# Moving 32 columns between the last two pieces of the last row of a ReLU row-sum

## The chip, the cores and the metric

The kernel runs on one core of one Trainium2 chip. The metric is the device time of one execution in microseconds; most numbers are medians over several executions. The profiler's own span, from the first to the last instruction, is about 1.4 us shorter than that time.

## The reference, cut to what matters

```python
x = np.random.randn(32, 512, 1024).astype(np.float32)     # 67.11 MB
out = np.sum(np.maximum(x, 0), axis=-1)                   # 32 x 512
```

There are 16384 rows of 1024 numbers. Each of the 128 partitions takes 128 rows.

## The kernel before: the parts that matter here

SP (SyncE) issues all loads: seven large chunks of 16 rows a partition, then the tail of 8, 4, 2 and 1 rows, and at last the last row in three pieces.

```python
TAIL = [8, 4, 2, 1]
LAST = [512, 256, 256]
...
n0, n1 = LAST[0], LAST[0] + LAST[1]
parts = [buf[:, tb, r, 0:n0], buf[:, tb, r, n0:n1], last[:, 0 : LAST[2]]]
for k, (lo, hi) in enumerate([(0, n0), (n0, n1), (n1, D)]):
    sp.dma_start(out=parts[k], in_=xv[-1][:, BIG - 1, lo:hi]).then_inc(...)
sp.wait_ge(s_fact, 1)                                      # the early store
sp.wait_ge(s_fdve, 1)
sp.dma_start(out=ov[1][:, :], in_=res[:, start[1] : start[2]]).then_inc(s_store, 16)
sp.wait_ge(s_turn, 1)
sp.dma_start(out=of[0:P]..., in_=turned[0:P:32, 0:32]).then_inc(s_store, 16)
```

ScalarE (ACT) sums the first piece and VectorE (DVE) the second. Each puts its partial sum into one of two extra columns behind the third piece, so that DVE's last sum adds the third piece and both partial sums in one instruction:

```python
n = LAST[2]
act.wait_ge(s_in[-3], 16)
on_act(parts[0], last[:, n : n + 1]).then_inc(s_part, 1)
dve.wait_ge(s_in[-2], 16)
on_dve(parts[1], last[:, n + 1 : n + 2]).then_inc(s_part, 1)
dve.wait_ge(s_part, 2)
dve.wait_ge(s_in[-1], 16)
on_dve(last[:, :], res[:, J - 1 : J]).then_inc(s_tdve, 1)
sp.wait_ge(s_tdve, 1)                                      # the final store
sp.dma_start(out=ov[-1][:, :], in_=res[:, start[-1] : J]).then_inc(s_out, 16)
```

## Time and profile before

| | before |
|---|---|
| time, median of 3 (range) | 160.97 us (160.97 to 161.2) |
| span in the profile | 159.9 us |
| read rate over the span | 420 GB/s |
| busy share of DVE and of ACT | 76% and 63% |
| end of the last sum to end of span | about 1.5 us |

The way to read it is from the end: the chain of work that ended last says which wait released the last sum, and the timeline of the last 3 us says how near the other waits were. The prediction below shows both, with its lines.

### The profile page before, as it was taken

The numbers are of one execution on the slowest core, as the hardware profiler recorded it, in microseconds if no ns is written. First come the engines' busy times: TensorE is split into PE (matmuls) and PEld (weight loads), VectorE is DVE, ScalarE is ACT, GpSimd is POOL, SyncE is SP. The second block draws the span as 40 slices with busy tenths as digits, with TensorE's granted clock in tenths as the row PEclk, the third lists the DMA queues.
The fourth block names the chain that finished last, engine by engine and source line by source line (L and its number), as shares of the span: only waits on it lengthen the run. The fifth ranks groups of instructions, "written<-read, shape, count | busy, mean of one in ns | idle before, by whom it ended". The sixth has DMA issues, their size and how long they took to land.

```text
span 159.9 us, 150 instructions
## 1 busy us (share of the span) xinstructions
DVE 121.5 (76%) x58; ACT 101.4 (63%) x55; POOL 0.2 (0%) x4
## 2 busy tenths in 40 slices
DVE  0000000999959999999969989699899999598995
ACT  3000059990799709996099942999339980496974
POOL 0000000000000000000000000000000000000000
DMA  9979996996996996997989969969969969899994
GB/s 377 492 338 400 492 525 262 525 525 262 525 525 262 525 525 262 525 459 328 525 361 426 525 262 525 525 262 525 525 262 525 525 262 525 369 418 393 408 381 148
DMA packets 2457, 67.18 MB, mean 420 GB/s; under 512 B 536, under 2 KB 792, under 8 KB 1176
## 3 DMA queue, kind: packets, MB, share of 16 engines
q1 hardware_dynamic: 2456, 67.18, 98.0%
q14 instruction: 1, 0.01, 0.0%
HBM read 67.11 MB, written 0.07 MB: 420 GB/s over the span
## 4 chain that ended last, share of the span: by engine, by line
DMA 68%; ACT 18%; DVE 11%; SPq 1%; issue 0%
DMA buf<-in_x_dram 68%; ACT buf L137 18%; DVE res L152 11%; SPq L98 1%; SPq L106 0%; DVE buf L122 0%; DVE last L122 0%
## 5 line engine op out<-in xcount | busy, mean ns | idle before, releaser
L152 DVE TENSOR_REDUCE res<-buf 128x7 f32<-128x7168 f32 (+4 forms) x16 | 100.0, 6281 | 33.7 <-ACT buf L137 33.7
L137 ACT ACTIVATE buf<-buf 128x7168 f32<-128x7168 f32 (+4 forms) x16 | 80.7, 5099 | 45.9 <-DMA buf<-in_x_dram 45.9
L119 ACT ACTIVATE buf<-buf 128x1024 f32<-128x1024 f32 (+1 forms) x19 | 19.0, 1000 | 9.3 <-DMA buf<-in_x_dram 9.3
L122 DVE TENSOR_SCALAR_CACHE_REDUCE buf<-buf 128x1024 f32<-128x1024 f32 (+2 forms) x19 | 20.9, 1147 | 3.1 <-DMA buf<-in_x_dram 2.9
L119 ACT ACTIVATION_READ_ACCUMULATOR buf<-buf 128x1 f32 x19 | 3.5, 186 | 0.0
L137 ACT ACT_TABLE_LOAD x1 | 1.3, 1283 | 1.3 <-PEq L216 1.3
L122 DVE DVE_READ_ACCUMULATOR buf<-buf 128x1 f32 x19 | 1.6, 84 | 0.0
L122 DVE TENSOR_SCALAR_CACHE_REDUCE last<-last 128x258 f32<-128x258 f32 x1 | 0.4, 422 | 0.0
L161 DVE STREAM_TRANSPOSE turned<-res 128x32 f32<-128x32 f32 x1 | 0.2, 211 | 0.0
L185 DVE TENSOR_TENSOR res<-half 128x1 f32<-128x1 f32 x1 | 0.2, 160 | 0.1
L216 POOL MEMSET const-bfloat16-1.0<- 128x1 bf16 x1 | 0.1, 102 | 0.0
L216 POOL MEMSET const-uint8-127<- 128x1 uint8 x1 | 0.1, 101 | 0.0
L216 POOL MEMSET const-float32-0.0<- 128x1 f32 x1 | 0.1, 99 | 0.2 <-issue 0.2
L216 POOL MEMSET const-float32-1.0<- 128x1 f32 x1 | 0.1, 98 | 0.0
L122 DVE DVE_READ_ACCUMULATOR last<-last 128x1 f32 x1 | 0.1, 83 | 0.0
## 6 DMA issues: line engine op xcount, KB each, us to landing
buf<-in_x_dram SPq DMA_DIRECT2D x1, 7680.0 KB, 21.2
buf<-in_x_dram SPq DMA_DIRECT2D x1, 4096.0 KB, 26.8
buf<-in_x_dram SPq DMA_DIRECT2D x1, 2048.0 KB, 31.3
buf<-in_x_dram SPq DMA_DIRECT2D x2, 512.0 KB, 18.9
buf<-in_x_dram SPq DMA_DIRECT2D x1, 1024.0 KB, 33.3
buf<-in_x_dram SPq DMA_DIRECT2D x1, 256.0 KB, 34.5
buf<-in_x_dram SPq DMA_DIRECT2D x1, 128.0 KB, 34.4
last<-in_x_dram SPq DMA_DIRECT2D x1, 128.0 KB, 34.2
```

What stands on the lines that cost most here:

```text
L98: sp.dma_start(out=buf[:, tb, r : r + n, :], in_=xv[-1][:, r : r + n, :]).then_inc(s_in[NBIG + i], 16)
L119: return act.activation(t, t, AF.Relu, accum_out=acc)
L122: return dve.tensor_scalar(out=t, in0=t, scalar1=0.0, scalar2=None, op0=ALU.max, op1=ALU.add, accum_out=acc)
L137: act.activation(t, t, AF.Relu).then_inc(s_act, 1)
L152: dve.tensor_reduce(out=res[:, c * BIG + r : c * BIG + r + n], in_=buf[:, c % NB, r : r + n, :], axis=X, op=ALU.add,).then_inc(s_dve, 1)
L161: dve.transpose(out=turned[:, :], in_=res[:, 0:32]).then_inc(s_turn, 1)
L185: dve.tensor_tensor(out=res[:, j0 + r : j0 + r + 1], in0=half[:, 0:1], in1=half[:, 1:2], op=ALU.add)
L216: nc = _bacc.Bacc("TRN2", target_bir_lowering=False, num_devices=1)
```

## The change

The intent is to let DVE begin and end its own part of the last row a little earlier, at the price of a longer last sum. That would pay if DVE's own part is what the last sum waits for.

```diff
-LAST = [512, 256, 256]
+LAST = [512, 224, 288]
```

## The prediction

> **What bounds the kernel now.** I read the page first, for its chain of work that ended last (part 4), then that chain in order of time, then the timeline of the last three microseconds, and last the groups of instructions with different shapes kept apart. The page gives the share of the whole span:
>
> ```profile
> ## 4 chain that ended last, share of the span: by engine, by line
> DMA 68%; ACT 18%; DVE 11%; SPq 1%; issue 0%
> ...
> HBM read 67.11 MB, written 0.07 MB: 420 GB/s over the span
> ```
>
> The reader is to see that the kernel is one stream of 67.11 MB. Its rate over the span of 159.9 us, 420 GB/s, is nearly the same in every stretch that I cut out of it (419 in the first 20 us, 446 from 40 to 80, 419 from 80 to 120), and the busy share of the 16 DMA engines is 97% to 103% in all of them up to 145 us. ACT (ScalarE) and DVE (VectorE) have idle time, 63% and 76% busy. So nothing that the change does can matter except in two places: the bytes (they stay the same) and the tail, after the stream has run dry. The end of the chain in order of time:
>
> ```profile
> 123.13 34.38 DMA buf<-in_x_dram
> 157.51 0.02 issue
> 157.53 0.44 DVE buf L122 x2
> 157.97 0.02 issue
> 158.00 0.43 DVE last L122 x2
> ```
>
> The columns are start, length and what, in us. The transfer that was issued at 123.13 is the second piece of the last row (256 columns). It lands at 157.51, DVE sums it in 0.44 us (the sum and the read of its accumulator), then sums the third piece in 0.43 us. After that only the store is left: issue at 158.45, landing 1.4 us later. The timeline of the same stretch shows who else could have held up that last sum:
>
> ```profile
> 157.17 0.63 ACT L119 ACTIVATE buf<-buf 128x512 f32<-128x512 f32 x1
> 157.27 0.16 DVE L185 TENSOR_TENSOR res<-half 128x1 f32<-128x1 f32 x1
> 157.53 0.42 DVE L122 TENSOR_SCALAR_CACHE_REDUCE buf<-buf 128x256 f32<-128x256 f32 x1
> 157.70 0.19 ACT L119 ACTIVATION_READ_ACCUMULATOR buf<-buf 128x1 f32 x1
> 157.88 0.08 DVE L122 DVE_READ_ACCUMULATOR buf<-buf 128x1 f32 x1
> 158.00 0.42 DVE L122 TENSOR_SCALAR_CACHE_REDUCE last<-last 128x258 f32<-128x258 f32 x1
> 158.34 0.08 DVE L122 DVE_READ_ACCUMULATOR last<-last 128x1 f32 x1
> 158.45 0.34 SPq L200 DMA_DIRECT2D out_dram<-res  x1
> ```
>
> The last sum, of 258 columns (256 of data and the two partial sums), needs three things. ACT's part of 512 columns is done at 157.70 + 0.19 = 157.89. DVE's own part is done at 157.96. The third piece was issued at 123.61 and took 34.2 us, by the page:
>
> ```profile
> last<-in_x_dram SPq DMA_DIRECT2D x1, 128.0 KB, 34.2
> ```
>
> so it landed at about 157.8 (the trace's landing record for its semaphore says 157.86). The three come within 0.1 us of each other, and DVE's own part is the last of them by 0.07 us. DVE itself was free at 157.27 + 0.16 = 157.43, so it stood for 0.1 us until the second piece landed.
>
> [...] So a column costs (1217 - 687)/512 = 1.035 ns and the number of instructions, not their cut, carries the rest.
>
> **The change, part by part.** The number of instructions, transfers and waits stays the same; 32 columns move from the second piece to the third.
>
> 1. The second piece is 112 KB where it was 128 KB. The first piece landed at about 122.64 + 34.5 = 157.14 and the second at 157.51, so 128 KB take 0.37 us there; 32/256 of that is 0.046 us. It should land at about 157.46. DVE is free since 157.43, so its sum can start at about 157.49 where it started at 157.53: 0.04 us earlier.
> 2. That sum is shorter by 32 x 1.035 = 33 ns: 0.44 becomes 0.41 us, and it is done at about 157.49 + 0.41 = 157.90.
> 3. ACT's part is untouched and done at 157.89, so this is now a dead heat.
> 4. The third piece ends the stream, and all bytes ahead of it are the same, so it lands when it did, 157.86. [...]
> 5. The last sum starts at the latest of the three, plus the 0.03 us that lay between 157.97 and 158.00: about 157.93 where it was 158.00. It has 290 columns where it had 258, so it is 33 ns longer: 0.43 becomes 0.46 us. It ends at about 158.39 where it ended at 158.43.
> 6. The store follows as before, 1.4 us.
>
> The sum: DVE's work on the two pieces together is the same 512 columns, so the 33 ns taken from one are given back in the other. What is left is only the earlier start, some **0.04 us** of 160.97, or 0.03%. I expect 160.93 us.
>
> **The rivals.** *First: another wait ends last and the gain is nothing or less.* If the third piece lands later than 157.90[...], the last sum waits for it, still being 33 ns longer. For a landing at 157.95 the end would be where it was; for one at 158.05, 0.1 us later. What speaks for it is that the piece is only about 0.1 us ahead of the sum now; what speaks against it is that the bytes up to its end are the same. Time: 160.95 to 161.1 us. *Second: ACT's part becomes the bound.* It is done at 157.89, so the last sum can't start before some 157.92 however fast DVE gets; that caps the gain at 0.08 us less the 33 ns, about 0.05, and a slightly late ACT takes it away. Time: 160.92 to 161.0. *Third: the second piece doesn't land earlier,* [...] Then DVE starts at 157.53 as before, and the two effects of 33 ns cancel exactly: 160.97. *Fourth: the stream itself moves,* since the buffer behind the last piece grows by 128 B a partition and shifts the small tiles. Nothing in the profile speaks for it; the rate is the same in every stretch.
>
> **Range and chances.** All rivals lie within 0.15 us of each other. The runs of the kernel before differ by 0.23 us (160.97 to 161.2), more than the whole effect, so it is this spread that makes the range: 160.6 to 161.35. For a change of 2% the time would have to move by 3.2 us. From 156.51, when the row before the three pieces has just landed and its sums start, to the end of the span there are only 3.4 us, 1.4 of them the store, and no step above is over 0.1 us. So within 2% is almost sure: 0.985, with 0.005 for faster and 0.01 for slower, for a disturbed run[...].
>
> **What the changed kernel's profile would show.** Step 1: the DVE sum of 224 columns starts at about 157.49 by the same clock, 0.04 earlier against the start of ACT's 512 columns; if it still starts 0.36 us behind that ACT instruction, the third rival holds. Step 2: it takes about 387 ns where 420 stood. Step 5: the last sum, 128x290, takes about 455 ns and starts within 0.05 us of the end of ACT's accumulator read. The chain should still end in DVE; should it name the transfer into the last tile as what released the last sum, the first rival holds, and should it name ACT, the second. The total may well show none of it. The prediction would be wrong if the last piece landed over 0.3 us later, or the load stream lost a third of a per cent of its rate.

The sum came to 0.04 us, from 160.97 to 160.93 us. The 1.035 ns of a column come from the sums in the trace, 420 ns with 256 columns, 687 with 512 and 1217 with 1024; by them each sum has an estimated 155 to 157 ns beside its columns.

## The result, and the profile after

The changed kernel took 161.05 us, the median of 6 runs (160.91 to 161.46), beside 160.97 for the kernel before (6 runs, 160.89 to 161.2). The ratio is 1.0007, with a 95% interval of 0.9994 to 1.0021: no difference that the runs can tell.

The profile shows a good deal more. This is the end of the chain, in order of time, for the changed kernel (start, length, what):

```profile
123.56 34.15 DMA last<-in_x_dram
157.71 0.03 issue
157.73 0.02 DVEq L195
157.75 0.07 issue
157.82 0.46 DVE last L122 x2
```

And this is its timeline, where the number in brackets is how long the engine stood, and for what:

```profile
156.15 0.69 DVE L122 TENSOR_SCALAR_CACHE_REDUCE buf<-buf 128x512 f32<-128x512 f32 x1
...
156.83 0.63 ACT L119 ACTIVATE buf<-buf 128x512 f32<-128x512 f32 x1
...
157.13 0.39 DVE L122 TENSOR_SCALAR_CACHE_REDUCE buf<-buf 128x224 f32<-128x224 f32 x1
157.36 0.19 ACT L119 ACTIVATION_READ_ACCUMULATOR buf<-buf 128x1 f32 x1
157.45 0.08 DVE L122 DVE_READ_ACCUMULATOR buf<-buf 128x1 f32 x1
157.82 0.46 DVE L122 TENSOR_SCALAR_CACHE_REDUCE last<-last 128x290 f32<-128x290 f32 x1 [0.30 <-DMA last<-in_x_dram]
...
158.31 0.34 SPq L200 DMA_DIRECT2D out_dram<-res  x1
```

Three things are to be seen. First, the parts did what was meant: the sum of 224 columns starts 157.13 - 156.15 = 0.98 us after the half-row sums, where the sum of 256 started 157.53 - 156.51 = 1.02 after them, and both partial sums are there by 157.55. Second, DVE then stood for 0.30 us, waiting for the third piece, which landed at 157.71. Before, that piece landed 0.35 us behind the second; here 0.59 us (from the trace's landing records: each of these loads has 16 increments of its semaphore there, those of the third piece of the changed kernel from 157.09 to 157.71, and I count it as landed with the last of them). Third, even after the landing it took 0.11 us to start, with an instruction of DVE's sequencer between (DVEq L195), where the kernel before needed 0.03 us from DVE's own part. The span is not longer for it (159.8 us beside 159.9), because the loads happened to be done sooner in this execution: the half-row sums started at 156.15 and not at 156.51. So I compare tails from the start of those half-row sums on. To the issue of the final store it is 158.45 - 156.51 = 1.94 us before and 158.31 - 156.15 = 2.16 us after.

Is the late third piece the change's doing or chance? And what is the 0.11 us?

### The profile page after: what moved, and what is told of

Its sections match the earlier page's. It is cut to its first block, busy times and chain, and to the rows that moved or that the text cites. A ratio compares the mean times of both kernels' runs of the same rounds, so it can differ in the third digit from the quotient of the medians.

```text
span 159.8 us, 150 instructions
## 1 busy us (share of the span) xinstructions
DVE 121.5 (76%) x58; ACT 101.4 (63%) x55; POOL 0.2 (0%) x4
## 4 chain that ended last, share of the span: by engine, by line
DMA 68%; ACT 18%; DVE 11%; SPq 2%; issue 0%; DVEq 0%
DMA buf<-in_x_dram 46%; DMA last<-in_x_dram 21%; ACT buf L137 18%; DVE res L152 11%; SPq L98 1%; SPq L106 1%; DVE last L122 0%; DVEq L195 0%
## 5 line engine op out<-in xcount | busy, mean ns | idle before, releaser
L122 DVE TENSOR_SCALAR_CACHE_REDUCE last<-last 128x290 f32<-128x290 f32 x1 | 0.5, 455 | 0.3 <-DMA last<-in_x_dram 0.3
```

The costliest lines, as they stand in the source:

```text
L122: return dve.tensor_scalar(out=t, in0=t, scalar1=0.0, scalar2=None, op0=ALU.max, op1=ALU.add, accum_out=acc)
```

## The experiments

### Both kernels again, and the two waits in the other order

The first two runs are the kernel before and the changed kernel, unedited. The other two have this edit, on the changed kernel (e3) and on the kernel before (e4):

```diff
-    dve.wait_ge(s_part, 2)
     dve.wait_ge(s_in[-1], 16)
+    dve.wait_ge(s_part, 2)
     on_dve(last[:, :], res[:, J - 1 : J]).then_inc(s_tdve, 1)
```

> The kernel before, unchanged, for a second look at its tail. In the first look the second piece landed at 157.51, the third 0.35 us later, and the last sum started at 158.00, 0.03 after DVE's own part. If the stretch from the landing of the last piece to the start of the last sum is set by DVE's own part, it is again 0.10 to 0.15 us. If the tail is a matter of chance from run to run, the distance of the two last landings is anywhere between 0.3 and 0.6 us here too.

> The changed kernel, unchanged. Theory 1 (the last sum now waits for the third piece, and that wait is an instruction of its own ahead of the sum): the sum starts 0.11 us after the landing wherever that lies, and the time is within 0.1 us of the kernel before. Theory 2 (the third piece lands late because its rows are longer[...]): it lands about 0.59 us behind the second piece again, where 0.35 + 0.05 would be the bytes alone. Theory 3 (chance): the distance falls back to about 0.40 us in this look.

> The changed kernel with the two waits ahead of the last sum in the other order, so that the wait for the third piece rides on the sum itself. Theory 1: the sum starts 0.03 us after the landing in place of 0.11, and the time is 0.08 us less than that of the changed kernel. Rival: the 0.11 us are the landing's own delay, then it stays at 0.11 and the time doesn't move.

> The kernel before with the two waits in the other order. Theory 1: the sum's own wait is then that for the piece, and that for the two parts is an instruction of its own. Where DVE's part comes last, as in the first look (157.97), the sum starts 0.11 behind it in place of 0.03: 0.08 us slower than before. Rival: no difference, the order of waits is free.

The kernel before, in its second look, had the late landing itself, and worse. The end of its chain:

```profile
123.80 34.49 DMA last<-in_x_dram
158.29 0.03 issue
158.31 0.02 DVEq L195
158.34 0.07 issue
158.41 0.43 DVE last L122 x2
```

Its third piece landed 0.88 us behind the second, and this one run took 161.67 us. The changed kernel, in its second look, had no late landing (0.34 us behind the second):

```profile
156.14 0.02 issue
156.17 1.42 ACT buf L119 x4
157.58 0.02 issue
157.61 0.46 DVE last L122 x2
```

Here ACT's four instructions (its half of the row before, its piece of the last row, and the two reads of accumulators) release the last sum, as the prediction's second rival had it. To the issue of the final store it is 1.93 us. Five runs of it gave 160.90 us (160.87 to 160.97), ratio 0.9994 (0.9982 to 1.0007). So the late landing comes and goes in both kernels: theory 2 (longer rows) falls and chance (theory 3) holds.

The waits. With the order swapped, e3 had a late landing again, but its last sum started 0.03 us after it; e4 had none, and its last sum started 0.12 us after DVE's own part. First the end of e3's chain, then that of e4's:

```profile
123.71 34.34 DMA last<-in_x_dram
158.05 0.02 issue
158.08 0.46 DVE last L122 x2
```

```profile
157.70 0.03 issue
157.73 0.02 DVEq L195
157.75 0.07 issue
157.82 0.43 DVE last L122 x2
```

The extra instruction follows the wait that is written second, in both kernels. Where that wait ended last, the last sum started 0.11 us (the changed kernel) and 0.12 us (e1, e4) after its release, and 0.03 us after it where the other did (the kernel before, e2, e3). So one of two waits costs some 0.09 us more, if it is the one that ends last. Theory 1 holds as to its cause. It doesn't show in the times: e3 took 161.08 us (160.91 to 161.37), ratio 1.0008 (0.9995 to 1.0020), where 0.08 us less than the changed kernel was expected, and e4 took 161.05 us (160.97 to 161.11), ratio 1.0002 (0.9989 to 1.0016). The late landing, which came in e3's profiled run too, is larger than what the wait saves: DVE stood 0.37 us for it in that run.

### What makes the third piece land late

The early store, 444 bytes (111 results) from each of 128 partitions, was issued at 147.26 in the kernel before, on the same queue as the loads (q1 in the profile) and long after the last of them (124). In that trace the third piece's packets ran up to 157.46 and the store's from 157.12 to 157.63: directly behind, with some overlap.

The packet records also say what is late, and it is not the data. From the end of the third piece's last packet to the last of its 16 increments it took 0.40, 0.47 and 0.44 us in the three profiles without a late landing so far (the kernel before, e4, e2), and 0.69, 1.04 and 0.87 us in the three with one (the changed kernel, e1, e3). In these, only the last two, six and one of the 16 increments were late.

I took that store away, with the small one issued behind it (e5 from the kernel before, e6 from the changed kernel; their output is wrong, and they serve for timing only). The expectation of e5 speaks of 127 rows' results; the two stores hold 111 and 1 a partition.

```diff
-    sp.wait_ge(s_fact, 1)
-    sp.wait_ge(s_fdve, 1)
-    sp.dma_start(out=ov[1][:, :], in_=res[:, start[1] : start[2]]).then_inc(s_store, 16)
-    sp.wait_ge(s_turn, 1)
-    sp.dma_start(out=of[0:P]..., in_=turned[0:P:32, 0:32]).then_inc(s_store, 16)
...
-    sp.wait_ge(s_store, 16 * (len(REGIONS) - 1))
```

and, for a version with right results, took both stores from SP in the same way and had ACT issue them (e7 with the changed cut, e8 with the cut of before; "ACT's queue" and "second queue" mean no more than that here):

```diff
+        if c == 3:
+            act.wait_ge(s_turn, 1)
+            act.dma_start(out=of[0:P]..., in_=turned[0:P:32, 0:32]).then_inc(s_store, 16)
...
+    act.wait_ge(s_fact, 1)
+    act.wait_ge(s_fdve, 1)
+    act.dma_start(out=ov[1][:, :], in_=res[:, start[1] : start[2]]).then_inc(s_store, 16)
     for r, n, s in tail[:-1]:
```

> The kernel before without the store of the first 127 rows' results and its wait (so most of the output is wrong, on purpose). In the trace that store's 444-byte packets run directly behind the third piece[...]. Theory (its writes hold up the third piece's last semaphore increments): the third piece lands 0.30 to 0.40 us behind the second, never 0.5 or more, the last sum starts 0.03 behind DVE's own part, and the scatter of the times shrinks; span 159.4 to 159.6 us in the profile. Rival (the late landings come from the loads themselves): landings 0.5 to 0.9 us apart still occur, and the scatter stays.

> The changed kernel without that store (output wrong on purpose), beside the kernel before without it: the change alone, freed of the late landings. The prediction's sum says 0.04 us faster than that kernel. [...]

> The changed kernel with the early stores issued by ACT[...], one in the middle of the run and one at about 147 us[...]; results right. Theory: no late landing of the third piece, time 160.7 to 160.9, and 0.1 to 0.2 us below the changed kernel on average. Rival (the store's bytes only move): same time as the changed kernel; or ACT loses the 0.4 us of issue in the tail and it is slower by up to that.

> The kernel before with the early stores on ACT's queue in the same way; results right. Theory: as the one with the changed cut, 160.7 to 160.9 us, within 0.05 us of it. Rival: same as the kernel before.

In none of the four did the third piece land late: 0.30, 0.35, 0.35 and 0.32 us behind the second, with the last increment 0.43 to 0.45 us after the last packet. The times scatter less: 160.84 to 161.05 (e5, 6 runs) and 160.87 to 161.11 (e6, 6 runs), where 11 runs of the kernel before on that chip went from 160.86 to 161.93. Both medians are 160.96 us, beside 161.02; the ratios are 0.9984 (0.9965 to 1.0004) and 0.9985 (0.9965 to 1.0005). With this quiet pair, the change can be read alone. The end of the timeline of the kernel before without the store, then of the changed one:

```profile
156.21 0.69 DVE L115 TENSOR_SCALAR_CACHE_REDUCE buf<-buf 128x512 f32<-128x512 f32 x1
...
157.26 0.42 DVE L115 TENSOR_SCALAR_CACHE_REDUCE buf<-buf 128x256 f32<-128x256 f32 x1
...
157.72 0.42 DVE L115 TENSOR_SCALAR_CACHE_REDUCE last<-last 128x258 f32<-128x258 f32 x1
...
158.18 0.35 SPq L193 DMA_DIRECT2D out_dram<-res  x1
```

```profile
156.15 0.69 DVE L115 TENSOR_SCALAR_CACHE_REDUCE buf<-buf 128x512 f32<-128x512 f32 x1
...
157.13 0.39 DVE L115 TENSOR_SCALAR_CACHE_REDUCE buf<-buf 128x224 f32<-128x224 f32 x1
...
157.59 0.46 DVE L115 TENSOR_SCALAR_CACHE_REDUCE last<-last 128x290 f32<-128x290 f32 x1
...
158.08 0.35 SPq L193 DMA_DIRECT2D out_dram<-res  x1
```

From the half-row sums, the last sum starts after 1.51 us with 256 columns and after 1.44 with 224: 0.07 us sooner. It is 0.03 us longer. To the issue of the store it is 1.97 and 1.93 us: a gain of 0.04 us. The pair on ACT's queue gives the same, 1.96 us (158.15 - 156.19) and 1.92 (158.21 - 156.29). The kernel before (1.94) against e2 (1.93), both without a late landing, gives only 0.01. Tails of one cut differ by a few hundredths from profile to profile, so a single pair settles nothing.

But the version on ACT's queue is no better in time: 161.20 us (e7, ratio 0.9998, 0.9976 to 1.0019) and 161.17 (e8, ratio 0.9999, 0.9979 to 1.0018), where 160.7 to 160.9 was expected. Its twelve runs lie within 161.10 to 161.30, with no outlier, but at a higher floor. The loss lies outside the span: the profiled runs took 161.24 and 161.20 us with spans of 159.68 and 159.61, a difference of 1.56 and 1.59 us. In the profiled runs of the kernel before, of e2, e5 and e6 it is 1.34 to 1.36 us. Over all twelve runs of e7 and e8 the difference goes from 1.3 to 1.6 us, 1.5 on average (their spans are on record to 0.1 us). The cause is not shown. One thing in the traces goes with it: e7 and e8 alone fetch a second block of 8 KB of instructions, 1.3 us after their last instruction.

### One queue, the store ahead of the small loads, and the cut moved further

The last group splits the results so that the early store holds 95 rows a partition in place of 111 and is issued ahead of the small loads, on the same queue. The core of the edit:

```diff
-REGIONS = [1, 111, 16]
+REGIONS = [1, 95, 32]
...
+    sp.wait_ge(s_dve, done[NTWO - 1])
+    sp.dma_start(out=ov[1][:, :], in_=res[:, start[1] : start[2]]).then_inc(s_store, 16)
     r = 0
     tail = []
     for i, n in enumerate(TAIL):
```

The four runs differ only in the cut: 512, 256, 256; 512, 224, 288; 512, 128, 384; 512, 320, 192.

> The cut of the kernel before (512, 256, 256), with the results split so that the early store holds only what is done by about 126 us and is issued ahead of the small loads, on the same queue; the final store takes 32 columns in place of 16; results right. Theory: no store behind the third piece, so no late landing, no second queue to pay for; the span is 159.4 to 159.6 and the time 160.8 to 161.0 with little scatter, 0.05 to 0.15 below the kernel before on average. From the start of the half-row sums to the end of the last sum it takes 1.94 us, as without the store. Rival: the wait ahead of the small loads or the wider rows of the last region cost more than is gained: 161.1 or more.

> The same with the cut of the change (512, 224, 288). Theory: from the start of the half-row sums to the end of the last sum 1.90 us, 0.04 less than with 256; the last sum is released by ACT's part. The time is 0.04 us below that one, which five rounds may not show. Rival: a landing that is late after all, then DVE's last sum is released by the third piece.

> The same with the change taken four times as far (512, 128, 384). DVE's own part is done long before; ACT's part, done when it always was, or the third piece sets the start of the last sum, so the start doesn't come earlier than with 224, while the sum is 96 columns or 0.10 us longer: 2.00 us from the start of the half-row sums to the end of the last sum, 0.06 more than with 256 and 0.10 more than with 224. Rival (DVE's part was the bound and stays the gain): 1.84 us or less.

> The same with the cut moved the other way (512, 320, 192). The second piece lands about 0.10 us later and takes 0.07 us longer, the last sum 0.07 us less: 2.04 us from the start of the half-row sums to the end of the last sum, 0.10 more than with 256; the last sum is released by DVE's own part. Rival (the third piece's landing bounds whatever the cut): 1.87 us, for a shorter last sum.

As a better kernel this is a plain miss: 163.28, 163.25, 163.42 and 163.10 us, with ratios of 1.0139, 1.0132, 1.0142 and 1.0125. The little scatter that was expected is not there either: the four runs of each lie within 0.35 to 0.68 us, so the store behind the third piece is not the only source of scatter. I had taken DVE to be done with the sixth chunk at 126 us, and it is done at 136. In the first of them the DMA queue's timeline is

```profile
136.11 0.34 SPq L102 DMA_DIRECT2D out_dram<-res  x1
136.51 2.25 SPq L106 DMA_DIRECT2D buf<-in_x_dram  x4
```

so the small loads were issued only when the queue was running dry, and from 135 to 140 us the core moved 154 GB/s, where the kernel before moved 380. For the tail alone the four are still a fair set, since all pay the same and none has a store behind the third piece. From the start of the half-row sums to the end of the last sum, with what the chain names as its release:

| cut | expected | measured | released by |
|---|---|---|---|
| 512, 320, 192 | 2.04 us | 1.96 us | DVE's own part |
| 512, 256, 256 | 1.94 us | 1.89 us | DVE's own part |
| 512, 224, 288 | 1.90 us | 1.87 us | ACT's part |
| 512, 128, 384 | 2.00 us | 2.02 us | ACT's part |

The last row is 160.15 + 0.56 - 158.69, from the end of its chain:

```profile
158.69 1.43 ACT buf L120 x4
160.12 0.03 issue
160.15 0.56 DVE last L123 x2
```

The order is the one that was expected, with the releases that were expected; the steps are 0.02 to 0.15 us where 0.04 to 0.10 were worked out. Each row is one profile. To the issue of the store, 256 columns took 1.92 to 1.97 us in four profiles without a late landing (the kernel before, e5, e8, e9; e4 is left out for its swapped waits) and 224 columns 1.90 to 1.93 in four (e2, e6, e7, e10), so the 0.02 us between these two rows alone would prove little; the larger steps are clear of that. Of the four cuts that were tried, 512, 224, 288 has the shortest tail, by 0.03 us on the average of those profiles. Taken further, DVE's own part is early for nothing and the last sum grows (0.56 us with 384 columns, 0.46 with 288). No version with right results is shown to be faster than both kernels.

## Why the prediction was right, point by point

**The bound** was right: the time is the stream of loads, and it is the same in both kernels (420 GB/s over the span in both profiles). The measured 161.05 us lies 0.12 us above the predicted 160.93 and within the range, and the change is the same within 2%. That says little for the 0.04 us: the range was set by the scatter of the runs, and the median lies 0.08 us above the kernel before, not 0.04 below it.

**Step 1** (the second piece lands earlier) was right with its size too small. Its landing came 0.35 to 0.37 us behind the first piece's in five profiles with 256 columns (the kernel before, e1, e4, e5, e8) and 0.29 to 0.31 in five with 224 (the changed kernel, e2, e3, e6, e7): 0.06 us, where 0.046 was estimated.

**Step 2** was right: 387 ns were expected and 385 measured in the profile of the changed kernel. **Step 3**, the dead heat, was nearly right: ACT's part became the release of the last sum in e2, e6, e7 and e10, so the second rival is what bounds the changed kernel when nothing is late.

**Step 4** failed, in the words "so it lands when it did", and the changed kernel's profile showed the sign of the first rival, the last sum released by the third piece. In three of six profiles with the early store behind it (the changed kernel, e1, e3) the third piece landed 0.59 to 0.88 us behind the second, where 0.30 to 0.35 was the rule, and it did so with either cut. In eight profiles without a store behind it, it never did (0.25 to 0.46 us). Three of six against none of eight could still be chance, by count about 1 in 18; that 4 of 11 runs of the kernel before took 161.3 us or more, and none of the twelve of e5 and e6 over 161.11, speaks for the store independently. So the first rival's effect came, but not by the length of the rows: the data came in time and the last increments late (in the changed kernel the last packet ended at 157.01, and the last increment came at 157.71). How the store holds those up was not observed. The cost for the place in the row at which the piece starts is shown by none of these runs: third pieces of 192 and 384 columns, from bytes 3328 and 2560 of the row on, landed 0.25 and 0.46 us behind the second piece (e12, e11), which puts a piece of 288 at an estimated 0.35 by a straight line, and those of 288, from byte 2944 on, came at 0.34, 0.35, 0.35 and 0.37 (e2, e6, e7, e10). Counted from the first piece's landing, the third comes after 0.63 to 0.64 us in all six.

**Step 5** was right where no landing was late: the last sum started 0.05 to 0.07 us sooner and lasted 0.03 us longer. It was wrong in its 0.03 us of start-up for a release by the landing: that is 0.11 us, because of the order of the two waits.

**The sum**, 0.04 us, is about what the tails show: 0.01 (the kernel before against e2), 0.04 (e5, e6), 0.04 (e8, e7) and 0.02 us (e9, e10). The times can't show it: the late landing alone moves a run by up to half a microsecond (in e1 the third piece landed 0.88 us behind the second, in the first look 0.35), and it comes to both kernels.

## What to carry to other kernels

When two engines and a transfer meet in one last instruction, list the three times at which they are done before moving work between them: here they lay within 0.1 us of each other (157.86, 157.89 and 157.96), so moving 32 columns could give no more than the distance to the next of them. Look at what is queued behind the last load as well (here the late landing came in three of six profiles with a store there, and in none of eight without), and at the order of the waits: here the last sum started 0.03 us after the release where the wait written first ended last, and 0.11 to 0.12 us where the other did. A change of 0.04 us, in runs that differ by 0.3 us, can be read only from distances within a trace, over several executions.
